# A two-layer hybrid decoder: x and mem handed over by channels, the first block's loads interleaved, and 512-wide token-major products

## The chip, the core and the metric

The kernel runs on one core of a Trainium2 chip. TensorE (PE) multiplies, VectorE (DVE), ScalarE (ACT) and GpSimd (POOL) work on tiles in SBUF and PSUM, and SyncE (SP) hands most loads and stores to the DMA queues. The metric is the device time of one execution in microseconds. The kernel before takes 1723.31 us, the median of three runs (1721.63 to 1724.03).

## The reference

The computation is a trunk of two layers over 512 tokens with 1024 channels. Each layer adds a mixer of the normalised h, and then a cross-attention to a memory of 256 tokens:

```
h = x
for l in range(DEPTH):
    un = _rmsnorm(h, mix_norm_g[l])
    h = h + _mixer_sublayer(un, ...)       # one projection w_in, four branches, gates, w_out
    xn = _rmsnorm(h, xa_norm_g[l])
    mn = _rmsnorm(mem, xa_mem_norm_g[l])
    h = h + _cross_attn(xn, mn, xa_wq[l], xa_wkv[l], xa_wo[l])
return _rmsnorm(h, final_norm_g)
```

The projection of a mixer is `z = un @ w_in`; its columns are cut into the inputs of RWKV-7 (r, k, v and low-rank codes), gated linear attention (GLA; q, k, v and a low-rank forget code of 16 columns behind v), retention (q, k, v) and a recurrent unit (LRU), and into the merge gates. `_rmsnorm` scales each token by `rsqrt(mean(x*x) + eps)` and each channel by a gain.

## The kernel before

**Layout.** h lives as eight tiles `hm` of 128 channels x 512 tokens. Every matrix and every activation that TensorE reads is split into two parts, a rounded one and the rest (`wh`, `wl` for weights; `uh`, `ul`, or `gh`, `gl`, for activations), and `mm3` (L309) issues three matmuls for one product: high x high (L313), and the two mixed ones (L314, L315). A weight is staged by an SP load into a tile `st`, ACT casts it into `wh` (L301), and DVE subtracts to make `wl` (L302). `wload` (L292) does that in two pieces per staged tile; three staged tiles fit at a time.

**Two ways of multiplying.** `proj` and `dense8` hold 128 weight columns in TensorE and stream 512 tokens. The token-major products hold 128 tokens and stream weight columns: `proj_tok` (L495) for the value inputs of GLA and retention (`gla_v`, `ret_v`), `v_proj` (L1321) for the values of the cross-attention, and `finish` (L1398) for the last `xa_wo` with the final norm. They stream 256 columns, in `gla_v` 264 (256 of v and 8 of the 16 code columns), so that a 512-column product is done in two halves, each with all eight channel blocks k.

**Start.** x arrives by tokens. SP loads ident (the unit matrix), the parameters, x's first 256 channels, the first staged weight, and on in turns. `first_rows` (L393) has TensorE transpose each channel block in four pieces (L414); ACT copies it with the gain into `uh` (L416), DVE makes the rest (L418) and the plain copy `hm` (L420), and ACT squares x and sums over channels for the token scale r. `bcast_cols` (L354) spreads r over the partitions: DVE multiplies it into ident (L359), TensorE multiplies that by `ones` (L361). In layer 0 that stands between the first and the second half of `gla_v`. The evacuations of `gla_v` (L520, L524 for the code columns) multiply by r as well. `flo_parts` (L528) transposes the code columns (L278, tile `m`). Then come `ret_v`, and the projections of the LRU in `mixers`.

**Layer 1.** h is there by channels; squares are summed on DVE, `rstd_finish` (L333) sums them over partitions on TensorE (L337) before `gla_v`.

**mem** is loaded by tokens in `load_mem` (L437), transposed by 16 matmuls on TensorE, scaled by its own r on DVE and written to a DRAM copy `mem_sc`, which the cross-attention of each layer reads back. h of each layer is written to DRAM (`h_sc`, eight stores) and read back for the residual after `w_out`.

**What sets the order.** A scheduler lays out the engines' queues from priorities: `tc.high_priority` pulls work ahead, `tc.issue_after(x)` holds an instruction's place behind x. In `rwkv_prep` (L940) long products of other branches are laid between the steps of a head pair j: `step(NST[i])` draws that many projections of 24 matmuls, and what follows is issued after the last of them. In a pair j the bonus (L1045, on `rkh` and `rkl` split by L322 and L323) comes first, then the transposes of v, then `step(NST[0])`.

## Time and profile before

| what | value |
|---|---|
| median of three runs | 1723.31 us |
| the profiled execution's own time | 1721.81 us |
| its span, first to last instruction | 1720.0 us |
| TensorE busy | 1692.2 us, 98% |
| DVE, ACT, POOL busy | 67%, 47%, 7% |
| data moved | 209 MB, 122 GB/s on average |

The profile's page gives each engine's busy time; its chain of work leads back from the last instruction to what released each step. The waits of an engine list its idle time by what ended it; windows give the busy time, the number of instructions (x) and the granted clock of stretches; a timeline lists single instructions with their start and length. Matmuls overlap, so the spacing from start to start, not the length of a row, is what one costs in a stream.

### The profile page before, as it was taken

Reading aid. Unit: us, or ns where it says so; the run is one execution under the profiler, and the core shown is the slowest. Engines: PE = TensorE matmul, PEld = TensorE weight load, DVE = VectorE, ACT = ScalarE, POOL = GpSimd, SP = SyncE. Lnnn points to the kernel's source line nnn. Section 1 sums busy time; section 2 is a strip of 40 time slices with the busy share of each in tenths; the row PEclk is TensorE's granted clock in tenths of the full one; section 3 lists DMA queues with packets and bytes.
Section 4 is the critical chain, followed back from the end, with each engine's and each line's share of the span. In section 5 each row is a group of like instructions: output and inputs, shape, how many; then the busy total and the mean of one; then the engine's idle time right before and its main releaser. Section 6 shows DMA issues by size and latency. Waiting matters only on the chain.

```text
span 1720.0 us, 27688 instructions
## 1 busy us (share of the span) xinstructions
PE 1692.2 (98%) x10570; PEld 1418.7 (82%) x10570; DVE 1147.7 (67%) x2369; ACT 810.0 (47%) x1539; POOL 114.2 (7%) x251
## 2 busy tenths in 40 slices
PE   7999999999999999999999999999999999999998
PEld 6987788877787788989898878887778878889898
DVE  7688577577775845756576737757878568557554
ACT  6494536454332334545446834545442234335354
POOL 1010000001003000000100100100110030000002
PEclk9999999999999999999999999999999999999999
DMA  6344325246562343424333424433547335334232
GB/s 218 98 134 124 99 81 165 88 114 173 159 174 88 118 155 99 135 87 130 108 102 87 128 73 137 123 93 104 152 131 210 99 96 186 92 97 134 86 104 81
DMA packets 320324, 209.17 MB, mean 122 GB/s; under 512 B 43616, under 2 KB 297792, under 8 KB 320192
## 3 DMA queue, kind: packets, MB, share of 16 engines
q1 hardware_dynamic: 310512, 189.71, 37.8%
q0 software_dynamic: 9680, 17.70, 3.6%
q8 instruction: 83, 1.36, 0.3%
q14 instruction: 49, 0.40, 0.1%
HBM read 176.97 MB, written 27.79 MB: 119 GB/s over the span
## 4 chain that ended last, share of the span: by engine, by line
PE 91%; DVE 6%; ACT 1%; DMA 1%; issue 1%; SPq 0%; POOL 0%; DVEq 0%; ACTq 0%; POOLq 0%
PE pb L313 25%; PE pb L315 25%; PE pb L314 25%; PE ps L278 2%; PE ps L313 2%; PE ps L315 2%; PE ps L314 2%; DVE wl L302 1%; PE ps L1069 1%; DVE sc L1037 1%; PE ps L1199 1%; PE ps L1205 1%; DVE sc L1036 1%; PE ps L784 1%; DVE R L1033 1%
## 5 line engine op out<-in xcount | busy, mean ns | idle before, releaser
L301 ACT CAST wh<-st 128x512 fp32r<-128x512 f32 (+1 forms) x548 | 339.6, 620 | 617.5 <-PE pb L314 502.8
L302 DVE TENSOR_TENSOR wl<-st,wh 128x512 fp32r<-128x512 f32 (+1 forms) x548 | 376.6, 689 | 339.3 <-ACT wh L301 300.1
L313 PE MATMUL pb<-uh,wh 128*128 128x512 f32 x1488 | 585.4, 394 | 0.0
L315 PE MATMUL pb<-uh,wl 128*128 128x512 f32 x1488 | 583.8, 392 | 0.0
L314 PE MATMUL pb<-ul,wh 128*128 128x512 f32 x1488 | 583.7, 392 | 0.0
L313 PEld LDWEIGHTS pb<-uh,wh 128*128 128x128 f32 x1488 | 280.1, 188 | 58.5 <-issue 1.6
L315 PEld LDWEIGHTS pb<-uh,wl 128*128 128x128 f32 x1488 | 279.6, 188 | 58.2 <-issue 0.3
L314 PEld LDWEIGHTS pb<-ul,wh 128*128 128x128 f32 x1488 | 279.7, 188 | 57.6 <-issue 0.8
L315 PE MATMUL pb<-yb,wl 128*128 128x512 f32 x256 | 101.3, 396 | 0.0
L313 PE MATMUL pb<-yb,wh 128*128 128x512 f32 x256 | 101.1, 395 | 0.0
L314 PE MATMUL pb<-yb,wh 128*128 128x512 f32 x256 | 100.1, 391 | 0.0
L315 PEld LDWEIGHTS pb<-yb,wl 128*128 128x128 f32 x256 | 48.0, 188 | 10.4
L313 PEld LDWEIGHTS pb<-yb,wh 128*128 128x128 f32 x256 | 48.1, 188 | 9.9
L314 PEld LDWEIGHTS pb<-yb,wh 128*128 128x128 f32 x256 | 48.1, 188 | 9.7
L914 DVE SCALAR_TENSOR_TENSOR bt<-bt,pb 128x512 f32<-128x512 f32 x48 | 32.9, 685 | 26.5 <-PE pb L315 26.2
L899 ACT ACTIVATE bt<-pb 128x512 f32<-128x512 f32 x64 | 38.0, 595 | 10.3 <-DVE hm L915 9.0
L313 PE MATMUL ps<-wh,R 128*128 128x256 f32 (+1 forms) x128 | 37.4, 292 | 0.2 <-DVE m L524 0.2
L314 PE MATMUL ps<-wl,R 128*128 128x256 f32 (+1 forms) x128 | 36.8, 288 | 0.0
L314 PE MATMUL pb<-wl,R 128*128 128x256 f32 (+1 forms) x128 | 36.7, 291 | 0.0
L314 PE MATMUL pb<-iv,wh 128*128 128x256 f32 x128 | 36.7, 286 | 0.0
L313 PE MATMUL pb<-wh,R 128*128 128x256 f32 (+1 forms) x128 | 36.5, 290 | 0.0
L313 PE MATMUL pb<-wh,uh 128*128 128x256 f32 x128 | 36.3, 284 | 0.0
(378 smaller groups left out, 2694.8 us busy)
## 6 DMA issues: line engine op xcount, KB each, us to landing
st<-in_w_in SPq DMA_DIRECT2D x154, 512.0 KB, 3.6
st<-in_w_branch SPq DMA_DIRECT2D x32, 512.0 KB, 3.5
st<-in_xa_wkv SPq DMA_DIRECT2D x32, 512.0 KB, 3.7
y_sc<-m POOLq DMA_DIRECT2D x32, 256.0 KB, 2.7
yb<-y_sc POOLq DMA_DIRECT2D x32, 256.0 KB, 4.9
st<-in_w_out SPq DMA_DIRECT2D x16, 512.0 KB, 3.5
st<-in_xa_wq SPq DMA_DIRECT2D x16, 512.0 KB, 3.4
st<-in_xa_wo SPq DMA_DIRECT2D x16, 512.0 KB, 4.0
```

Of the source, the lines that this page charges most:

```text
L278: PE.transpose(o, i, idn)
L301: S.copy(hi, st[:, i * n:(i + 1) * n])
L302: V.tensor_tensor(lo, st[:, i * n:(i + 1) * n], hi.bitcast(F32), op=ALU.subtract)
L313: PE.matmul(o, ah, bh, start=first and i == 0, stop=False)
L314: PE.matmul(o, ah, bl, start=False, stop=False)
L315: last_mm[0] = PE.matmul(o, al, bh, start=False, stop=last and i == n - 1)
L784: PE.matmul(ops[q][:, j], atts[q][:, j], v[:, b, h * P:(h + 1) * P], start=j == 0, stop=b == 0, skip_group_check=True)
L899: S.activation(t, o, AF.Tanh, scale=0.5)
L914: V.scalar_tensor_tensor(th[d], th[d], 1.0, o, op0=ALU.add, op1=ALU.mult)
L1033: V.scalar_tensor_tensor(dst[:, :, 1:], c8(kn[qs])[:, :, 1:], -1.0, c8(pp[qs])[:, :, :63], op0=ALU.mult, op1=ALU.mult)
L1036: V.scalar_tensor_tensor(b2[qs, :, q], c8(aa[qs]), 0.5, c8(cum[qs]), op0=ALU.mult, op1=ALU.mult)
L1037: V.tensor_tensor(b2[qs, :, 1 - q], c8(km[qs]), c8(cum[qs]), op=ALU.mult)
```

## The change

The host hands over x and mem transposed (`xt`, `memt`), so that the transposes of x (32) and of mem (16) and the copies out of PSUM fall away. At the start SP gives out the parameters, then in turns one channel block of x (256 KB, straight into its `hm` tile) and a piece of the first staged weights, cut by `FIRST_W`; ACT and DVE split them in the same order. ident and the constants come after these. While the data are on the way TensorE multiplies a tile of ones 11 times; its memset is POOL's first, ahead of the load of `heads`. The squares for r are taken after the splits, and r is made (`rstd_finish`) in the middle of the second half of `gla_v` in both layers; `proj_tok` evacuates both halves behind all its matmuls, and the spreading of r comes behind `proj_tok`. `tok_major` streams 512 columns for `ret_v`, `v_proj` and the first half of the last `xa_wo`. mem's scaling stands in `rwkv_prep`. h of layer 0 isn't written out: the residual is read from `xt`. `NST` has one projection of 24 matmuls ahead of the bonus, and four in place of five behind it. The tile `dec` is wider, which moves addresses only.

```diff
+FIRST_W = {0: 1, 1: 1, 2: 2, 4: 2, 6: 2}
-NST = (5, 1)
+NST = (1, 4, 1)
...
+        for k in range(KD):
+            n = FIRST_W.get(k)
+            if n:
+                nc.sync.dma_start(first_w[k // 4][:, k % 4:k % 4 + n], a["w_in"][0][k * P:(k + n) * P, ...
+            nc.sync.dma_start(xs[k], a["xt"][k * P:(k + 1) * P])
     cst = cp.tile([P, NCST], F32, name="cst")
+    nc.sync.dma_start(ident, a["ident"])
     nc.sync.dma_start(cst, a["consts"])
...
+    with tc.high_priority(offset=100000):
+        G.memset(ones, 1.0)
+        warm = pss((P, P))
+        for _ in range(11):
+            PE.matmul(warm, ones, ones, start=True, stop=True)
     heads = cp.tile([P, P + 134 + T], F32R, name="heads")
...
+    def tok_major(w, xh, xl, nb):
+        parts = [wload(w[q * 256:(q + 1) * 256], 2, T) for q in range(4)]
+        os_ = [pb() for _ in range(nb)]
+        for k in range(KD):
+            hi, lo = (x[k % 2] for x in parts[k // 2])
+            for b in range(nb):
+                bs = slice(b * P, (b + 1) * P)
+                mm3(os_[b], [(xh[k][:, bs], xl[k][:, bs], hi, lo)], first=k == 0, last=k == KD - 1)
+        return os_
...
+        with tc.high_priority(offset=100000):
+            for k in range(KD):
+                n = FIRST_W.get(k)
+                if n:
...
+                    chain("S", lambda: S.copy(wh[:, ws], st))
+                    chain("V", lambda: V.tensor_tensor(wl[:, ws], st, wh[:, ws].bitcast(F32), op=ALU.subtract))
+                chain("S", lambda: S.activation(hi[k], h[k], AF.Copy, scale=gcol[:, k:k + 1]))
+                chain("V", lambda: V.scalar_tensor_tensor(lo[k], h[k], gcol[:, k:k + 1], hi[k].bitcast(F32),
+                                                          op0=ALU.mult, op1=ALU.subtract))
+        acc = None
+        with tc.issue_after(last["S"].ins):
+            for k in range(KD):
+                acc = add_square(acc, h[k], T)
+        return hi, lo, lambda: rstd_finish(acc, T, D), parts
...
+            for bg in ((0, 1, 2), (3,)) if half else ((0, 1, 2, 3),):
+                os_ += [(pss if half else pb)((P, wd)) for _ in bg]
+                for k in range(KD):
+                    for b in bg:
+                        bs = slice(b * P, (b + 1) * P)
+                        mm3(os_[b], [(gh[k][:, bs], gl[k][:, bs], parts[k // 4][0][k % 4], parts[k // 4][1][k % 4])],
+                            first=k == 0, last=k == KD - 1)
+                    if half and k == 3 and callable(r):
+                        with tc.issue_after(last_mm[0].ins):
+                            r = r()
...
+                mm = step(NST[0])
                 bon = pss()
-                for x in (rkh, rkl):
-                    PE.matmul(bon, same, x, start=x is rkh, stop=x is rkl)
+                with tc.issue_after(mm):
+                    for x in (rkh, rkl):
+                        PE.matmul(bon, same, x, start=x is rkh, stop=x is rkl)
...
-        for k in range(KD):
-            nc.sync.dma_start(h_sc[l][:, k], h[k])
-        if l:
+        else:
+            for k in range(KD):
+                nc.sync.dma_start(h_sc[:, k], h[k])
             gh, gl, r = gain_split(h, g_)
-        rp = bcast_cols(r, T)
-        v_gla, ex = proj_tok(l, COL["gla_v"], gh, gl, r, extra=16, staged=(None, None) if l else first_w)
+            ready = None
+        v_gla, ex, r = proj_tok(l, COL["gla_v"], gh, gl, r, extra=16, ready=ready)
+        with tc.issue_after(last_mm[0].ins):
+            rp = bcast_cols(r, T)
         fl = flo_parts(ex)
         xh, xl = norm_split(h, g_, rp)
-        v_ret = proj_tok(l, COL["ret_v"], gh, gl, r)
+        for b, o in enumerate(tok_major(a["w_in"][l][:, COL["ret_v"]:COL["ret_v"] + T], gh, gl, 4)):
...
-            nc.sync.dma_start(old, h_sc[l][:, d])
+            nc.sync.dma_start(old, h_sc[:, d] if l else a["xt"][d * P:(d + 1) * P])
```

On TensorE the kernel before begins with the transposes of x (`R_73`, `R_74` are x's loaded tiles, `R_117` and `R_119` the two parts of x, `pb_259` and on the sums of the four token blocks):

```order
L1527 UNCONDITIONAL_BRANCH
L414 MATMUL ps_121<-ident,R_73 128x128 x4
L414 MATMUL ps_129<-ident,R_73 128x128 x4
L414 MATMUL ps_137<-ident,R_74 128x128 x4
L414 MATMUL ps_145<-ident,R_74 128x128 x4
L313 MATMUL pb_259<-wh_243,R_117 128x264
L314 MATMUL pb_259<-wl_244,R_117 128x264
```

In the changed kernel it begins with the multiplied ones (`R_131` and `R_133` are the two parts of x there, and L312 to L314 the three matmuls of `mm3`):

```order
L1552 UNCONDITIONAL_BRANCH
L222 MATMUL ps_105<-ones 128x128 x11
L312 MATMUL pb_195<-wh_135,R_131 128x264
L313 MATMUL pb_195<-wl_136,R_131 128x264
L312 MATMUL pb_196<-wh_135,R_131 128x264
L313 MATMUL pb_196<-wl_136,R_131 128x264
```

The products of ones stand where the transposes stood; nothing of x is needed for them.

At the end of `gla_v` and the start of `ret_v` the kernel before had 17 matmuls on TensorE between the first three transposes of the code columns (`m_241`, one per token block) and the fourth, of which these are the last:

```order
L315 MATMUL pb_568<-wh_550,R_119 128x256
L313 MATMUL pb_569<-wh_550,R_117 128x256
L314 MATMUL pb_569<-wl_551,R_117 128x256
L278 MATMUL ps_491<-ident,m_241 96x128
L315 MATMUL pb_569<-wh_550,R_119 128x256
```

In the changed kernel the spreading of r (L371) stands ahead of them, and the fourth transpose of the code columns (`m_193`) comes after four matmuls of `ret_v`:

```order
L371 MATMUL ps_440<-m_435,ones 128x512
L278 MATMUL ps_442<-ident,m_193 96x128 x3
L312 MATMUL pb_539<-wh_501,R_131 128x512
L313 MATMUL pb_539<-wl_502,R_131 128x512
L314 MATMUL pb_539<-wh_501,R_133 128x512
L312 MATMUL pb_540<-wh_501,R_131 128x512
L278 MATMUL ps_442<-ident,m_193 96x128
L313 MATMUL pb_540<-wl_502,R_131 128x512
```

DVE makes that fourth block of `m_193` in the last row of the following piece (L301 there makes `wl`, L536 and L540 are the evacuations of `gla_v`, the operations on `ti_657` small steps of `derive`, which makes constants from the parameters):

```order
L540 TENSOR_SCALAR m_193<-ps_317,ti_359 128x3x16
L268 TENSOR_SCALAR ti_657<-ti_657 128x4
L267 TENSOR_TENSOR ti_657<-ti_657,ti_656 128x4
L268 TENSOR_SCALAR ti_657<-ti_657 128x4
L267 TENSOR_TENSOR ti_657<-ti_657,ti_656 128x4
L301 TENSOR_TENSOR wl_502<-st_499,wh_501 128x512
L268 TENSOR_SCALAR ti_657<-ti_657 128x4
L301 TENSOR_TENSOR wl_506<-st_499,wh_505 128x512
L267 TENSOR_TENSOR ti_657<-ti_657,ti_656 128x4
L301 TENSOR_TENSOR wl_512<-st_509,wh_511 128x512
L536 TENSOR_SCALAR R_192<-ps_398,ti_359 128x248
L301 TENSOR_TENSOR wl_516<-st_509,wh_515 128x512
L540 TENSOR_SCALAR m_193<-ps_398,ti_359 128x3x16
```

In the kernel before the same place on DVE read:

```order
L524 TENSOR_SCALAR m_241<-ps_385,ti_221 128x3x16
L368 SCALAR_TENSOR_TENSOR m_541<-hm_116,par_78,ps_238 128x512
L302 TENSOR_TENSOR wl_551<-st_548,wh_550 128x512
L302 TENSOR_TENSOR wl_555<-st_548,wh_554 128x512
L520 TENSOR_SCALAR R_240<-ps_386,ti_221 128x248
L302 TENSOR_TENSOR wl_561<-st_558,wh_560 128x512
L302 TENSOR_TENSOR wl_565<-st_558,wh_564 128x512
L524 TENSOR_SCALAR m_241<-ps_386,ti_221 128x3x16
```

The four splits for `ret_v` stood there already, between the third and the fourth block of the code columns; the steps of `derive` stood behind these rows, and now stand ahead of and among them.

## Rows read from the trace of the kernel before

**Rows 1.** Page: busy by engine with share; the chain that ended last.

```profile
PE 1692.2 (98%) x10570; PEld 1418.7 (82%) x10570; DVE 1147.7 (67%) x2369; ACT 810.0 (47%) x1539; POOL 114.2 (7%) x251
PE 91%; DVE 6%; ACT 1%; DMA 1%; issue 1%; SPq 0%; POOL 0%; DVEq 0%; ACTq 0%; POOLq 0%
```

**Rows 2.** Waits of PE: line, what it waited for: us, times, longest.

```profile
PE ps L414 <- DMA R<-in_x: 8.0, 2, 7.0
PE ps L361 <- DVE m L359: 3.5, 1, 3.5
PE ps L1045 <- DVE m L323: 3.1, 7, 0.9
PE ps L1045 <- ACT m L322: 2.4, 4, 0.7
PE ps L337 <- POOL m L330: 0.9, 1, 0.9
```

**Rows 3.** Windows, start: PE, PEld, DVE, ACT, POOL busy (x); clock, DMA, GB/s.

```profile
7.00:11.50 4.50, 3.50 (x16) 3.12 (x17) 2.41 (x4) 2.73 (x5) 0.00 (x0) 1.00 1.10 353
...
13.50:25.90 12.40, 12.40 (x105) 12.30 (x103) 10.91 (x20) 11.21 (x42) 0.42 (x1) 1.00 0.96 306
25.90:29.60 3.70, 0.15 (x2) 0.07 (x1) 2.76 (x19) 3.50 (x4) 0.00 (x0) 1.00 0.85 269
29.60:33.80 4.20, 4.20 (x17) 3.63 (x18) 3.67 (x8) 2.81 (x6) 0.00 (x0) 0.59 0.70 198
...
44.30:55.90 11.60, 11.60 (x100) 11.60 (x99) 8.80 (x34) 3.92 (x8) 0.00 (x0) 1.00 0.49 136
55.90:67.50 11.60, 11.60 (x99) 11.60 (x98) 5.27 (x9) 4.41 (x9) 0.00 (x0) 1.00 0.33 92
```

**Rows 4.** Windows of later stretches, columns as in Rows 3.

```profile
72.00:152.00 80.00, 80.00 (x358) 65.88 (x357) 68.61 (x112) 64.81 (x95) 5.29 (x10) 1.00 0.40 112
590.00:690.00 100.00, 100.00 (x443) 82.80 (x442) 57.70 (x94) 38.88 (x67) 0.00 (x0) 1.00 0.42 129
1672.50:1710.50 38.00, 38.00 (x319) 38.00 (x319) 16.64 (x40) 16.84 (x45) 9.87 (x12) 1.00 0.16 52
```

**Rows 5.** Timeline of SP's issues at the start: start, length.

```profile
1.67 0.43 SPq L198 DMA_DIRECT2D R<-in_x  x1
```

**Rows 6.** Timeline of ACT, start; in brackets the idle time before.

```profile
8.42 1.16 ACT L301 CAST wh<-st 128x528 fp32r<-128x528 f32 x2 [6.39 <-DMA st<-in_w_in]
...
11.10 0.69 ACT L416 ACTIVATE R<-ps,par 128x512 fp32r<-128x512 f32 x1 [0.34 <-PE ps L414]
```

**Rows 7.** Timeline of DVE beside `ret_v`, layer 0.

```profile
48.34 0.69 DVE L302 TENSOR_TENSOR wl<-st,wh 128x512 fp32r<-128x512 f32 x1
...
49.34 0.16 DVE L267 TENSOR_TENSOR ti<-ti,ti 128x4 f32<-128x4 f32 x1
49.54 0.17 DVE L268 TENSOR_SCALAR ti<-ti 128x4 f32<-128x4 f32 x1
```

**Rows 8.** Timeline of PE in retention, layer 0: four f32 matmuls, two records each.

```profile
237.69 1.16 PE L784 MATMUL ps<-R,m 128*128 128x128 f32 x8
```

**Rows 9.** Timeline of PE: the sum for r in layer 1 (four f32 matmuls).

```profile
869.24 1.05 PE L337 MATMUL ps<-ones,m 128*128 128x1 f32 x8 [0.89 <-POOL m L330]
```

**Rows 10.** Timeline of PE: the bonus of j = 0, layer 0.

```profile
328.05 0.50 PE L1045 MATMUL ps<-m,heads 128*128 128x512 f32 x1 [0.52 <-ACT m L322]
```

**Rows 11.** Timeline of PE: transposes of mem between matmuls, two of eight pairs.

```profile
251.58 0.38 PE L278 MATMUL ps<-ident,hm 128*128 128x128 f32 x2
251.72 0.48 PE L313 MATMUL pb<-uh,wh 128*128 128x512 f32 x1
...
252.50 0.42 PE L278 MATMUL ps<-ident,hm 128*128 128x128 f32 x2
```

**Rows 12.** Window in GLA, layer 0, columns as in Rows 3.

```profile
166.90:170.30 3.40, 3.40 (x15) 2.30 (x14) 1.45 (x5) 0.00 (x0) 0.00 (x0) 0.50 0.00 0
```

More of the change, by code (lines that the diff above doesn't have):

```diff
@@ L192, in trunk_kernel @@
     ident = cp.tile([P, P], F32, name="ident")
-    with tc.high_priority(offset=100000):
-        nc.sync.dma_start(ident, a["ident"])
-    xs = [Rt((P, 4, 256)) for _ in range(4)]
-    def load_x(i):
-        nc.sync.dma_start(xs[i], a["x"][:, i * 256:(i + 1) * 256].rearrange("(b p) d -> p b d", p=P))
-    with tc.high_priority(offset=100000):
-        load_x(0)
+    xs = [ht() for _ in range(KD)]
     par = [cp.tile([P, NPAR], F32, name=f"par{l}") for l in range(depth)]
@@ L229, in spread @@
         return heads[:, (j + 1) * P + 134:(j + 2) * P + 134]
-    ones = cp.tile([P, P], F32, name="ones")
-    G.memset(ones, 1.0)
     reset = cp.tile([P, T], F32, name="reset")
@@ L406, in chain @@
                 last[eng] = f()
-            return last[eng]
-        for k in range(KD):
-            uh, ul = gh[k // 4][:, k % 4], gl[:, k] if k < 4 else yb()
-            with tc.high_priority(offset=100000):
-                tp = pss()
-                for b in range(4):
-                    chain("PE", lambda: PE.transpose(
-                        tp[:, b * P:(b + 1) * P], xs[k // 2][:, b, (k % 2) * P:(k % 2 + 1) * P], ident))
-                acts.append(chain("S", lambda: S.activation(uh, tp, AF.Copy, scale=gcol[:, k:k + 1])))
-            with tc.high_priority(offset=WPRI - 500):
-                chain("V", lambda: V.scalar_tensor_tensor(ul, tp, gcol[:, k:k + 1], uh.bitcast(F32), op0=ALU.mult,
-                                                          op1=ALU.subtract))
-                chain("V", lambda: V.tensor_copy(hT[k], tp))
-            hi.append(uh)
-            lo.append(ul)
@@ L504, in proj_tok @@
             G.memset(ex, 0.0)
+        halves = []
         for half in range(2):
             c0 = half * wd
-            n = min(wd, T - c0)
-            parts = [wload(w_in[q * 512:(q + 1) * 512, col + c0:col + c0 + wd], 4, wd, None if half else staged[q])
-                     for q in range(2)]
-            os_ = [(pss if half else pb)((P, wd)) for _ in range(4)]
-            for k in range(KD):
-                for b in range(4):
-                    bs = slice(b * P, (b + 1) * P)
-                    mm3(os_[b], [(gh[k][:, bs], gl[k][:, bs], parts[k // 4][0][k % 4], parts[k // 4][1][k % 4])],
-                        first=k == 0, last=k == KD - 1)
+            parts = ready if ready and not half else \
+                [wload(w_in[q * 512:(q + 1) * 512, col + c0:col + c0 + wd], 4, wd) for q in range(2)]
+            os_ = []
+            for bg in ((0, 1, 2), (3,)) if half else ((0, 1, 2, 3),):
[8 more added lines that the diff above has]
+                            r = r()
+            halves.append(os_)
+        for half, os_ in enumerate(halves):
+            c0 = half * wd
+            n = min(wd, T - c0)
             for b in range(4):
@@ L1050, in rwkv_prep @@
                 for w in range(4):
-                    transpose(ta[:, w], vt[:, w * P:(w + 1) * P], ident)
+                    with tc.issue_after(mm):
+                        transpose(ta[:, w], vt[:, w * P:(w + 1) * P], ident)
                 s0, s1 = c8(sv[:, j % 2, 0]), c8(sv[:, j % 2, 1])
@@ L1273, in step @@
             return last_mm[0].ins
-        rwkv_prep()
+        rwkv_prep(mem_scale)
         rwkv_invert()
```

145 lines of the change are left out of this document (70 added, 75 removed).

## The prediction

> **What bounds the kernel now.** I read the page first, then TensorE's waits, then windows of the stretches that the change touches, and single instructions in a timeline where a size was missing. TensorE is busy for 1692.2 us of a span of 1720.0, and the chain that ended last lies on it for 91% [rows 1]. All its recorded waits of some size are few: 8.0 us for x at the start, 3.5 for the spreading of r between the halves of `gla_v`, 5.5 in eleven waits for the bonus, 0.9 for the sum for r in layer 1 [rows 2]. So a change gains what it takes off TensorE's queue, in matmul time or in these waits, and nothing elsewhere, unless it brings a new wait. Busy time hides one more loss, half speed: the 16 transposes of x took 3.50 us, 0.22 each, while a pair of such transposes amid mem's projections adds about 0.24 (below); and behind the wait of 3.55 us the granted clock is 0.59 over 4.2 us, in which 17 matmuls ran where 36 would at the 105 in 12.4 us of the stretch before [rows 3]. The profiled execution took 1721.81 us, 1.5 below the median of the runs; I make the sum against 1721.8.
>
> **A. The start, up to the LRU's projection at 67.5 us.** Before: transposes from 7.03, the first matmul of `gla_v` at about 11.5, its first half to 26, the wait, r's spreading, the second half to 44.3, `ret_v` to 67.5 [rows 2, 3]. After, step by step.
>
> *First data.* SP gave out the first block of x at 1.67 and PE had it at 7.03 [rows 2, 5], behind ident, parameters and 512 KB. The new first block, parameters, 132 KB of weights and 256 KB of x, is 190 KB less, which at 353 GB/s [rows 3] is 0.5 us: 6.5 at the latest. If the time from issue to landing halves with the block, it is 4.4. I take 5.3. ACT's copy with gain costs 0.69 [rows 6], so data are ready at 6.0.
>
> *Multiplied ones.* 11 f32 matmuls need no data. Four such in full speed take 1.16 us [rows 8], 0.29 each, and twice that at half speed: 3.2 or 6.4 us in all. From about 1.5 us (an estimate: POOL's memset comes just before) they end at 4.7 to 7.9. Since PE came from idling here as it did at 7.03 and at 29.6, I take mostly half speed, 7.2. That is later than the data, and costs about 1 us; in turn the matmuls behind start near full speed.
>
> *First half.* 96 matmuls of 264 columns, at 12.4/105 = 0.118 [rows 3]: 11.3 us, to 18.5 (17.3 to 19.6). Per channel block that is 1.42 us of TensorE against 388 KB, 1.10 us at 353 GB/s, and ACT's 0.69 for x and, per block, half to all of a cast of 0.58 [rows 6]: TensorE is the slowest of the three, though not by much.
>
> *Sum for r in the second half.* 1.05 us [rows 9] of TensorE, new in layer 0; its squares, eight on ACT behind the last split, should end some 3 us before it is wanted. Second half: 11.3 more, to 30.8. The wait of 3.5 us and the half speed behind it are gone, because the spreading of r comes behind `proj_tok`: 0.85 us (an estimate from two 512-wide matmuls at 0.226 [rows 4] and transposes of code columns), to 31.7 with the code columns at 32.0.
>
> *A new wait.* The fourth transpose of the code columns now has four matmuls of `ret_v` ahead of it, not 17. DVE makes its data behind four splits of 0.69, an evacuation and the steps of `derive` at 0.2 each [rows 7]. If DVE starts these steps when r is known and the constants have been looked up on ACT, at about 26, its queue stands at 32.8 for the first split and at 36 for the fourth block. PE waits 0.5 to 4 us; I take 2.5. Behind PE's wait stands all of `ret_v`.
>
> *`ret_v`.* 96 matmuls of 512 columns at 100.0/443 = 0.226 [rows 4]: 21.7 us where 192 of 256 took 23.2 [rows 3]. So the LRU starts at 32.0 + 2.5 + 21.7 = 56.2: **11.3 us gained.** With the best of each piece it is 15; with the worst, and the half speed of rows 3 once more behind the new wait (2.1 us), 6.4.
>
> **B. 512 columns in the four other places** (`ret_v` of layer 1, `v_proj` of both layers, half of the last `xa_wo`). Each is 96 matmuls of 512 in place of 192 of 256. The stretch of 256-wide ones ran at 38.0/319 = 0.119, the 512-wide at 0.226 [rows 4]: two narrow ones cost 0.0125 more than a wide one, 1.2 us a place, 4.8. In `v_proj` both sums now end together, so the evacuations of the last one bunch; I take off 0.5: **4.3** (1 to 5). The weights' bytes and casts are the same. ACT and DVE have slack there (57.7 and 38.9 of 100 us busy [rows 4]).
>
> A rule speaks against this. The Trainium skill, page "TensorE: Matmul & The Clock Gate", section "Back-to-back issue gap", gives 262 cycles for 256 columns and 518 for 512; two narrow ones would then lose 6 cycles, 2.5 ns, and a place 0.24 us. The trace doesn't agree for the narrow ones (119 ns, not 109). If only the stretch at 1672 us were slow for a reason of its own, the sum would come out by the page's rule; that is a rival below.
>
> **C. The bonus of j = 0.** By the order, 48 long matmuls stand ahead of it in place of 37 and 13 behind it in place of 24; for j = 1 to 3 nothing moves. One wait there was 0.52 [rows 10], the second product adds its own, and a quarter of 5.5 us [rows 2] is 1.4 for both layers: **1.4** (0 to 2). The 11 matmuls moved ahead take 2.5 us, more than any one wait of 0.9.
>
> **D. mem's transposes.** From one pair to the next it is 0.92 us with three long matmuls between, 0.68 at 0.226: 0.12 a transpose [rows 4, 11]. Sixteen: **1.9**.
>
> **E. r in layer 1.** The wait of 0.9 [rows 2] goes, since the sum stands some 130 matmuls later: **1.0** (0.5 to 1.3); the sum's own 1.05 stays.
>
> **At nothing:** the eight stores of h in layer 0 and the residual from `xt` (DMA share 0.4 [rows 4], and both ends of them far from any wait); ident and the constants behind x (wanted at some 23 us); mem's scaling in `rwkv_prep` (eight DVE steps of 0.3 to 0.7 us; the copy is read hundreds of us later; without cover they would cost 3); `heads` 0.2 us later; `dec`.
>
> **Sum:** 11.3 + 4.3 + 1.4 + 1.9 + 1.0 = 19.9, so 1721.8 - 19.9 = **1701.9** (1703.4 if counted from the median of the runs). With the ends of the ranges: 1697 to 1711.
>
> **Rivals.** *The new wait at its worst, with half speed behind it:* A is 6.4, 1706.8. For it: the order on DVE; against: one may find `derive`'s steps long done. *The loads come no earlier* (smaller blocks in turns need as long as one large one, since all queues share 353 GB/s already [rows 3]), so the change doesn't do what it says at the start: the first block at 7.0 as before and blocks in the pace of loads of 1.10 to 1.5 us; A is about 9, 1704.2. *Narrow ones cost no more than half of wide ones* (the gap of 0.0125 us isn't the width's): B is 1.0 and A 1.0 less, 1706.2; that is the page's rule above. *The gain is given back behind:* between 72 and 152 us DVE is busy for 68.6 of 80 us and ACT for 64.8 [rows 4], PE never waits, but all of the squares, splits and loads come 11 us closer together; if DVE was only just ahead there, PE waits for weights, and A comes to nothing: 1713, and worse if the stretch costs 5 more. *Better than I think:* 15 for A, no wait in C, and the half speed in GLA at 167 us (clock 0.50 over 3.4 us [rows 12]) not met again, 1.7: 1721.8 - 15 - 4.3 - 2 - 1.9 - 1.0 - 1.7 = 1696. *Slower:* TensorE stays at half speed through the start, because waits for blocks recur. Each us of half speed costs 0.5. `gla_v`'s 192 matmuls would take 0.22 in place of 0.118, 19.6 more, and `ret_v` 21.7 more: 1743. It turns the sign from some 40 us of half speed, of the 50 there are. Against it: in the trace full speed came back within 4.2 us of steady matmuls after the wait of 3.5 [rows 3].
>
> **How the numbers follow.** Forecast 1701.9 (own range 1697 to 1706): 0.60. New wait at its worst, 1707: 0.14. Loads no earlier, 1704: 0.08. Width without gain, 1706: 0.05. Given back, 1713: 0.05, of it 0.02 within 0.2%. Better, 1696: 0.05. Half speed, 1743: 0.03. A difference of 0.2%, 3.4 us, is about what a measurement of this kernel can tell from no change. Faster by more than that: 0.95; within: 0.02; slower: 0.03. The range 1695 to 1710 leaves out the half speed, most of the given back and the tails.
>
> **What would show it.** A: the first `mm3` on PE at 6 to 8 us, 96 matmuls in about 11.4 us behind it, no gap between the halves, a wait of PE at the fourth transpose of code columns (for DVE, 0.5 to 4 us), the first LRU matmul at 56 us. A first matmul after 8.5, or gaps of PE for x or weights between blocks, would show the loads as the bound. B: 96 wide matmuls in 21.7 us each time. C: no wait at the bonus of j = 0, the others as before. D: no transposes of `hm` near 250 us. E: no wait at the sum in layer 1. It would be wrong if the granted clock fell in the start, if waits for `wl` showed up from 60 to 150 us, or if POOL, DVE or ACT were found ahead of PE in places where the trace of before has none.

## The result

The changed kernel takes **1702.79 us**, the median of four runs (1701.36 to 1705.67), beside 1723.67 us of the kernel before on the same chip (1721.63 to 1725.10). The ratio is 0.9882, 95% interval 0.9864 to 0.9900: faster by 1.2%, inside the range of 1695 to 1710 and within 1 us of the forecast 1701.9. The profiled execution took 1701.36 us, with a span of 1699.6 us against 1720.0.

The page's first line and its chain, which answer to [rows 1]: TensorE works 13 us less and is busy for 99% of the shorter span; of the chain that ended last it has 88%, DVE 7%.

```profile
PE 1679.0 (99%) x10072; PEld 1388.9 (82%) x10072; DVE 1142.6 (67%) x2344; ACT 805.3 (47%) x1496; POOL 113.5 (7%) x251
...
PE 88%; DVE 7%; ACT 2%; DMA 1%; issue 1%; SPq 0%; DVEq 0%; ACTq 0%
```

TensorE's waits in the changed kernel (line, what it waited for: us, times, longest), which answer to [rows 2]:

```profile
PE ps L1065 <- DVE m L333: 4.8, 8, 0.9
PE pb L312 <- ACT R L423: 1.6, 1, 1.6
PE ps L1065 <- ACT m L332: 1.3, 2, 0.7
PE ps L986 <- ACT m L332: 1.3, 2, 0.7
PE ps L278 <- DVE m L540: 1.1, 1, 1.1
PE ps L222 <- POOL ones L218: 1.0, 1, 1.0
```

The wait for x (8.0 us) has shrunk to 1.0 + 1.6; those for the spreading of r and for the sum for r in layer 1 are gone. The waits for the bonus (now L1065) are as large as before, 6.1 against 5.5. Two are new: 1.1 for the code columns (L278), which the prediction had, and 1.3 at L986, which it had not. L986 is the sum of squares of RWKV's keys in `rwkv_prep`, and it waits for ACT's part of a split, a rounded copy from which DVE then makes the rest.

To see where time went, I read the start of a few matmuls that both kernels have from each profile's timeline, and take the distances. The marks are, in each layer, the first matmul of GLA's gate (L612 in the changed kernel), the last of retention (L806), the first that spreads the norms of the keys in `rwkv_prep` (L1039) and the first of `rwkv_invert` (L1162); "RWKV's pairs" lies between the last two. The rows below the second are runs of the next section. Lengths in us; the last column is the span:

| kernel | start to GLA's gate | GLA, retention | to spreading in RWKV | RWKV's pairs | to GLA's gate, layer 1 | GLA, retention | to spreading | RWKV's pairs | to the end | span |
|---|---|---|---|---|---|---|---|---|---|---|
| before | 116.8 | 124.2 | 77.8 | 192.9 | 453.5 | 120.8 | 74.3 | 192.9 | 366.8 | 1720.0 |
| changed | 105.3 | 121.2 | 76.1 | 192.9 | 450.4 | 120.9 | 75.0 | 192.9 | 364.9 | 1699.6 |
| changed, again | 105.1 | 124.3 | 76.9 | 193.0 | 450.4 | 120.9 | 75.1 | 193.0 | 364.9 | 1703.4 |
| narrow | 107.7 | 124.5 | 76.0 | 193.0 | 452.7 | 120.8 | 74.3 | 193.0 | 367.0 | 1708.9 |
| bonus as before | 105.2 | 124.1 | 76.5 | 192.9 | 450.4 | 120.9 | 74.7 | 193.0 | 365.0 | 1702.8 |
| mem by tokens | 106.4 | 124.1 | 78.7 | 192.9 | 450.3 | 120.9 | 76.2 | 192.9 | 365.1 | 1707.6 |

So the gain of 20.4 us of span is 11.5 in the start, 3.0 in layer 0's GLA, 1.7 up to RWKV, 3.1 between the layers, 1.9 at the end, and minus 0.7 ahead of RWKV in layer 1. RWKV's pairs, in which the bonus lies, gave nothing. The 3.0 in GLA was not in the sum, only in the rival "better than I think"; the first experiment is about it.

TensorE's timeline at the start of the changed kernel (start, length, in brackets the idle time before):

```profile
1.00 4.12 PE L222 MATMUL ps<-ones 128*128 128x128 f32 x22 [1.00 <-POOL ones L218]
6.76 0.39 PE L312 MATMUL pb<-wh,R 128*128 128x264 f32 x1 [1.64 <-ACT R L423]
...
10.46 0.39 PE L314 MATMUL pb<-wh,R 128*128 128x264 f32 x1 [0.28 <-DVE R L424]
...
23.42 0.95 PE L347 MATMUL ps<-ones,m 128*128 128x1 f32 x8
...
31.60 1.03 PE L371 MATMUL ps<-m,ones 128*128 128x512 f32 x2
32.47 0.49 PE L278 MATMUL ps<-ident,m 128*96 128x128 f32 x3
...
34.99 0.31 PE L278 MATMUL ps<-ident,m 128*96 128x128 f32 x1 [1.11 <-DVE m L540]
...
56.01 0.39 PE L312 MATMUL pb<-uh,wh 128*128 128x512 f32 x1
```

The ones end at 5.1, the first product of `gla_v` starts at 6.76 behind ACT, r's sum (23.42) and its spreading (31.60) stand amid matmuls without a wait, and the LRU starts at 56.01, where it started at 67.5. In windows (busy time and instructions of PE, PEld, which is TensorE's loading of the stationary tile, DVE, ACT, POOL; clock, DMA share, GB/s), to set beside [rows 3]:

```profile
6.76:19.06 12.30, 12.02 (x97) 11.81 (x98) 11.41 (x18) 11.56 (x20) 0.42 (x1) 1.00 1.00 345
19.06:31.60 12.54, 12.54 (x106) 12.54 (x105) 9.60 (x45) 8.27 (x16) 0.00 (x0) 1.00 0.38 108
32.70:56.00 23.30, 22.19 (x100) 18.09 (x99) 19.20 (x38) 11.03 (x19) 0.00 (x0) 1.00 0.43 124
```

In the first window all three engines and the loads are all but full (ACT 11.56, DVE 11.41 of 12.30, 345 GB/s): the first half of `gla_v` lies near three bounds at once.

### The profile page after: what moved, and what is told of

Its sections match the earlier page's. It is cut to its first block, busy times and chain, and to the rows that moved or that the text cites. A ratio compares the mean times of both kernels' runs of the same rounds, so it can differ in the third digit from the quotient of the medians.

```text
span 1699.6 us, 26626 instructions
## 1 busy us (share of the span) xinstructions
PE 1679.0 (99%) x10072; PEld 1388.9 (82%) x10072; DVE 1142.6 (67%) x2344; ACT 805.3 (47%) x1496; POOL 113.5 (7%) x251
## 4 chain that ended last, share of the span: by engine, by line
PE 88%; DVE 7%; ACT 2%; DMA 1%; issue 1%; SPq 0%; DVEq 0%; ACTq 0%
PE pb L312 25%; PE pb L314 25%; PE pb L313 25%; DVE wl L301 2%; PE ps L278 2%; PE ps L312 1%; PE ps L314 1%; PE ps L313 1%; ACT wh L300 1%; PE ps L1090 1%; DVE sc L1055 1%; PE ps L1220 1%; PE ps L1226 1%; DVE R L1051 1%; PE ps L800 1%
## 5 line engine op out<-in xcount | busy, mean ns | idle before, releaser
L301 DVE TENSOR_TENSOR wl<-st,wh 128x512 fp32r<-128x512 f32 (+1 forms) x544 | 374.6, 689 | 332.9 <-ACT wh L300 294.2
L312 PE MATMUL pb<-uh,wh 128*128 128x512 f32 x1488 | 585.2, 393 | 0.0
L314 PE MATMUL pb<-uh,wl 128*128 128x512 f32 x1488 | 583.0, 392 | 0.0
L312 PEld LDWEIGHTS pb<-uh,wh 128*128 128x128 f32 x1488 | 280.1, 188 | 58.6 <-issue 1.4
L314 PEld LDWEIGHTS pb<-uh,wl 128*128 128x128 f32 x1488 | 279.5, 188 | 58.7 <-issue 0.3
L314 PE MATMUL pb<-yb,wl 128*128 128x512 f32 x256 | 101.3, 396 | 0.0
L312 PE MATMUL pb<-yb,wh 128*128 128x512 f32 x256 | 101.2, 395 | 0.0
L314 PEld LDWEIGHTS pb<-yb,wl 128*128 128x128 f32 x256 | 48.1, 188 | 10.4
L312 PEld LDWEIGHTS pb<-yb,wh 128*128 128x128 f32 x256 | 48.1, 188 | 9.9
L312 PE MATMUL pb<-wh,R 128*128 128x512 f32 (+1 forms) x128 | 43.2, 338 | 1.6 <-ACT R L423 1.6
L313 PE MATMUL pb<-wl,R 128*128 128x512 f32 (+1 forms) x128 | 43.1, 337 | 0.0
L314 PE MATMUL pb<-wh,R 128*128 128x512 f32 (+1 forms) x128 | 42.7, 337 | 0.3 <-DVE R L424 0.3
L314 PE MATMUL pb<-sc,wl 128*128 128x256 f32 x128 | 36.2, 283 | 0.0
L312 PE MATMUL pb<-sc,wh 128*128 128x256 f32 x128 | 36.2, 283 | 0.0
```

The lines of the kernel that those rows point to most:

```text
L301: V.tensor_tensor(lo, st[:, i * n:(i + 1) * n], hi.bitcast(F32), op=ALU.subtract)
L312: PE.matmul(o, ah, bh, start=first and i == 0, stop=False)
L313: PE.matmul(o, ah, bl, start=False, stop=False)
L314: last_mm[0] = PE.matmul(o, al, bh, start=False, stop=last and i == n - 1)
```

## The experiments

Each kernel is the changed one with the edit shown, and was run beside the kernel before.

**The changed kernel again.** No edit.

> The changed kernel once more, beside the others of this call. In its first profile the granted clock did not fall in layer 0's GLA, while it did in the kernel before and in four variants of the changed one that share every instruction there, at a cost of 2.9 us. Theory: that fall comes and goes between executions of one kernel and is no effect of the change; here the span is either near 1699.7 or near 1702.5, and the profiled execution shows which goes with it. Rival: the change removed it, and the four variants brought it back by their different start; then this run shows full clock there again, as the first.

1705.35 us, ratio 0.9896 (0.9873 to 0.9920). The windows of layer 0's GLA, first in the changed kernel's first profile, with the clock behind POOL's column:

```profile
150.00:156.00 6.00, 5.39 (x67) 3.52 (x66) 5.95 (x18) 3.72 (x5) 1.10 (x2) 1.00 0.63 176
156.00:160.00 4.00, 4.00 (x33) 2.85 (x33) 1.60 (x4) 0.75 (x4) 0.00 (x0) 1.00 0.33 131
160.00:164.00 4.00, 4.00 (x39) 3.10 (x38) 0.00 (x0) 2.13 (x11) 0.60 (x2) 1.00 0.02 4
```

and in this run of the same program:

```profile
150.00:156.00 6.00, 5.18 (x66) 3.53 (x66) 5.93 (x18) 3.72 (x5) 1.11 (x2) 1.00 0.65 176
156.00:160.00 4.00, 4.00 (x20) 3.11 (x20) 1.59 (x4) 0.00 (x0) 0.00 (x0) 0.52 0.32 131
160.00:164.00 4.00, 4.00 (x23) 2.60 (x22) 0.00 (x0) 1.81 (x10) 0.60 (x2) 0.62 0.02 4
```

The same instructions, once at full clock (2.4 GHz) and once at 0.52, that is at half of it (1.2 GHz) for nearly all of the window, behind a stretch in which PE is idle for 0.6 and 0.8 of 6 us. The rival (the change removed the fall) is out: the fall comes and goes between executions of one program. It costs 3.1 us here (124.3 against 121.2). The kernel before had it in its profile [rows 12]. With the fall in both, the change gains 1720.0 - 1703.4 = 16.6 us. Of the 3.8 us by which the first comparison shows more, 3.1 are the clock and 0.8 a shorter wait at the keys' sum of squares in layer 0 (0.7 us there, 1.5 in this run); both differ between executions of one program, so they are luck. The fastest execution of the kernel before that was measured beside any of these kernels took 1717.81 us, 16.5 more than the changed kernel's fastest, 1701.36.

**Without the multiplied ones.**

```diff
-        warm = pss((P, P))
-        for _ in range(11):
-            PE.matmul(warm, ones, ones, start=True, stop=True)
```

> The changed kernel without its 11 multiplied ones at the start; nothing else differs. Theory: in the profile of the changed kernel the first product of gla_v began at 6.76 us, after a wait of 1.6 us for ACT's first part of x, so the products of ones delay nothing; what they give is the clock. Without them the first matmuls of gla_v run at half speed (0.22 in place of 0.12 us each) for some 5 us, so the LRU's projection starts 2 to 3.5 us later than at 56.0, and the time is 2 to 3.5 us longer. Rival: the ones give nothing (matmuls of gla_v come up to speed by themselves, or the loads are the bound of the first half): within 0.7 us of the changed kernel.

1703.52 us, ratio 0.9890 (0.9874 to 0.9907); GLA's gate at 106.1, 0.8 to 1.0 behind the changed kernel's two. The theory's 2 to 3.5 is out; the rival's 0.7 holds nearly. The timeline of its first matmuls:

```profile
6.75 0.59 PE L309 MATMUL pb<-wh,R 128*128 128x264 f32 x1 [6.75 <-ACT R L420]
7.13 0.42 PE L310 MATMUL pb<-wl,R 128*128 128x264 f32 x1
```

They begin at the same 6.75 and run at half speed (0.22 from start to start further on) until 9.9, which costs some 1.4 us (an estimate: 14 matmuls at 0.10 more each); the changed kernel runs at full speed there, but in its first profile loses part of that in a wait (10.46 above). And the ones do not bring full speed each time. Of twelve profiles of kernels that have them, seven run the first block at full speed and five at half speed up to 10.2 to 10.8, the kernel "narrow" for one:

```profile
1.01 5.06 PE L222 MATMUL ps<-ones 128*128 128x128 f32 x22 [1.01 <-POOL ones L218]
7.00 0.59 PE L312 MATMUL pb<-wh,R 128*128 128x264 f32 x1 [0.92 <-ACT R L423]
7.38 0.42 PE L313 MATMUL pb<-wl,R 128*128 128x264 f32 x1
```

Those five reach GLA's gate about 1.2 us later than the seven where nothing else differs (106.4 against 105.0 to 105.3). Beside 106.1 without the ones, they gain 0.8 to 1.1 us where they bring full speed and lose 0.3 where they don't, with one profile of the kernel without them.

**256 columns in place of 512.**

```diff
-    def tok_major(w, xh, xl, nb):
-        parts = [wload(w[q * 256:(q + 1) * 256], 2, T) for q in range(4)]
-        os_ = [pb() for _ in range(nb)]
+    def tok_major(w, xh, xl, nb, c):
+        parts = [wload(w[q * 512:(q + 1) * 512, c * 256:(c + 1) * 256], 4, 256) for q in range(2)]
+        os_ = [(pss if c else pb)((P, 256)) for _ in range(nb)]
...
```

> The changed kernel with 256 streamed columns in the five places that stream 512 (ret_v twice, v_proj twice, half of the last xa_wo): twice as many matmuls, weights loaded in the shapes of the kernel before. Theory: two narrow matmuls cost 0.0125 us more than a wide one, 1.2 us for 96 pairs, so 5 to 6 us longer in all, 1.2 of it in ret_v of each layer. Rival: a narrow matmul costs about half a wide one (the page's cycles: 0.24 us a place), 1 to 2 us longer. A third: the wider shape changed how early weights come, and the difference is not in the spacing of matmuls but in waits.

1710.43 us, ratio 0.9931 (0.9916 to 0.9946), 5.4 to 6.9 above the three other kernels that ran beside it. By stage: the start is 1.2 longer than in "mem by tokens", which shares its half speed there; between the layers 2.3 more (`v_proj` and `ret_v`), at the end 2.1 more (`v_proj` and `xa_wo`): 5.6 in five places, 1.1 each. The windows amid `ret_v`, of "narrow" and then of the changed kernel:

```profile
37.50:55.00 17.50, 17.50 (x148) 17.50 (x147) 16.19 (x31) 9.54 (x18) 0.00 (x0) 1.00 0.40 105
```

```profile
36.00:55.00 19.00, 19.00 (x85) 15.73 (x85) 15.13 (x30) 9.37 (x17) 0.00 (x0) 1.00 0.43 125
```

17.5/148 = 0.118 and 19.0/85 = 0.224: two narrow ones cost 0.013 us more than a wide one. PEld is full in the narrow stretch (17.50 of 17.50) and not in the wide one (15.73 of 19.00), so the loads of the stationary tile are the likely bound of the narrow form; that is read, not tried.

The Trainium skill, page "TensorE: Matmul & The Clock Gate", section "Back-to-back issue gap", gives 262 and 518 cycles for the two widths, by which the five places would cost 1.2 us (an estimate: 6 cycles a pair at 2.4 GHz). The runs don't agree with the Trainium skill's cycles: 0.118 us for 256 columns where these make 0.109, and 0.224 for 512 where they make 0.216.

**The bonus as before, and one projection later.**

```diff
-                mm = step(NST[0])
                 bon = pss()
-                with tc.issue_after(mm):
-                    for x in (rkh, rkl):
-                        PE.matmul(bon, same, x, start=x is rkh, stop=x is rkl)
+                for x in (rkh, rkl):
+                    PE.matmul(bon, same, x, start=x is rkh, stop=x is rkl)
...
-                mm = step(NST[1])
+                mm = step(5)
```

> The changed kernel with the bonus as in the kernel before: no projection ahead of it, five behind. Theory: the wait at the bonus of j = 0 (1.1 us in both kernels) is for DVE's rest of the split, which the scheduler sets behind that pair's whole preparation; moving the bonus by 11 matmuls of TensorE's queue moved only what stands between its first and its second product, so going back changes nothing: within 0.5 us, the wait again in two parts of about 0.6 and 0.3 at j = 0 of both layers. Rival, my forecast: the move takes 0.7 us off each layer, so going back costs 1.4 us.

The second kernel has `NST = (2, 3, 1)`.

> The changed kernel with two projections (48 matmuls) ahead of the bonus and three behind. Theory: the second product of the bonus keeps its place on TensorE, where the scheduler thinks DVE's split done, and DVE's split stands no earlier; the wait of some 1.1 us at j = 0 stays in each layer: within 0.5 us of the changed kernel. Rival: one more projection of 5.4 us covers what was short: about 2 us less.

1704.76 us (ratio 0.9904, 0.9889 to 0.9918) and 1705.06 us (0.9901, 0.9886 to 0.9915). RWKV's pairs take 192.9 to 193.0 us in both layers of both kernels, as in the kernel before and in the changed one. The theory holds. The waits of TensorE for the bonus, of "bonus as before":

```profile
PE ps L1063 <- DVE m L333: 3.0, 6, 0.9
PE ps L1063 <- ACT m L332: 2.4, 4, 0.7
```

and of the one with two projections ahead:

```profile
PE ps L1065 <- DVE m L333: 5.3, 8, 1.1
PE ps L1065 <- ACT m L332: 1.3, 2, 0.7
```

As more work goes ahead, the wait changes its name from ACT to DVE and keeps its size or grows a little: 5.4, 6.1 in the changed kernel, 6.6. The changed kernel's timeline at j = 0 of layer 0, PE and then DVE:

```profile
317.19 0.39 PE L312 MATMUL pb<-uh,wh 128*128 128x512 f32 x1
318.50 0.50 PE L1065 MATMUL ps<-m,heads 128*128 128x512 f32 x1 [0.93 <-DVE m L333]
```

```profile
317.04 0.69 DVE L1055 TENSOR_TENSOR sc<-m,m 64x512 f32<-64x512 f32 x1
317.76 0.69 DVE L333 TENSOR_TENSOR m<-m,m 128x512 fp32r<-128x512 f32 x1
```

The bonus needs two products. The first, on ACT's part, was moved; the second waits for DVE's rest (L333), which stands last in the pair's preparation (it starts 0.03 us after L1055 ends). In the kernel before it stood there too, and so did the second product: 28 matmuls of TensorE lay between first and second, 17 in the changed kernel, 5 in the one with two projections ahead.

**Mem by tokens.**

```diff
-            nc.sync.dma_start(mT[i], a["memt"][2 * i * P:(2 * i + 2) * P].rearrange("(k p) m -> p k m", p=P))
+            nc.sync.dma_start(ms[i], a["mem"][(i // 2) * P:(i // 2 + 1) * P, (i % 2) * T:(i % 2 + 1) * T])
...
+                transpose(tp[:, b * P:(b + 1) * P], ms[2 * b + k // 4][:, (k % 4) * P:(k % 4 + 1) * P], ident)
+            V.tensor_copy(mT[k // 2][:, k % 2], tp)
```

> The changed kernel with mem handed over by tokens as in the kernel before: 16 transposes on TensorE and eight copies on DVE again, the scaling left in its new place. Theory: 16 x 0.12 = 1.9 us more between retention's end and the first bonus in layer 0; elsewhere nothing. Rival: part of it is hidden, because a wait near it (at the sum of squares of the keys, 0.7 us) shrinks by as much: 1.2 us.

One run of 1709.44 us. The stage from retention to RWKV's spreading is 78.7 us, against 76.9 in the changed kernel's second profile, 1.8 more, and 76.1 in its first, 2.6 more; without the waits of TensorE in that stage (1.1, 1.5 and 0.7) it is 2.1 to 2.2 more than either. In layer 0 the theory holds and the rival doesn't. The theory's "elsewhere nothing" is not what came: in layer 1, where no transpose of mem stands, the stage is 1.2 longer (76.2 against 75.0 and 75.1), because TensorE waits 1.8 us at the keys' sum of squares in place of 0.6 and 0.7; that wait is taken up below.

**The weights whole.**

```diff
-FIRST_W = {0: 1, 1: 1, 2: 2, 4: 2, 6: 2}
+FIRST_W = {0: 4, 4: 4}
...
```

> The changed kernel with the first weights loaded whole (528 KB ahead of x's first block, 528 KB ahead of its fifth), not in turns with x. Theory: 396 KB more stand ahead of the first block of x, 1.1 us at 353 GB/s, and another 132 KB's worth of splits on ACT and DVE ahead of its part; the first matmul of gla_v comes 1.1 to 2 us later than at 6.7, and since all bytes are the same and the loads are nearly the bound, part of it is made up by the end of the first half (19.1 us): the LRU starts 0.5 to 2 us later. Rival: the order of loads within a full queue changes nothing, within 0.3.

One run of 1709.68 us. The first product, from its timeline:

```profile
7.55 0.59 PE L312 MATMUL pb<-wh,R 128*128 128x264 f32 x1 [2.37 <-ACT R L423]
```

The first is at 7.55, where the other eleven with the ones have it from 6.76 to 7.21. The block runs at half speed, so it is compared with the others that do: GLA's gate is at 106.86 against 106.42 and 106.45 in two of them. That is 0.4 us, between the theory's 0.5 to 2 and the rival's 0.3, while profiles of one program lie 0.2 apart there: the interleaving counts for less than half a microsecond, and one profile shows no more. Of the rest of its time 3 us are luck: the clock fell in layer 1's GLA too (124.2 and 123.9 in the two layers).

**r between the halves.**

```diff
-                    if half and k == 3 and callable(r):
+                    if not half and k == KD - 1 and callable(r):
```

> The changed kernel with r made between the two halves of gla_v (in both layers), not in the middle of the second. Theory: the first half ends at 19.1 us and the squares' sum is done at about 22.8, so PE waits 3.7 to 4 us in layer 0, and behind that wait runs at half speed for some 4 us, which costs 2 more; in layer 1 nothing. LRU's projection 5.5 to 6.5 us later than in the changed kernel, the time as much longer. Rival: without half speed 3.7 to 4.

1710.87 us, ratio 0.9928 (0.9906 to 0.9949); GLA's gate at 111.0, 5.7 behind. The theory holds. PE's timeline, then the windows behind the wait, with the clock (0.50 and 0.73):

```profile
23.23 1.86 PE L347 MATMUL ps<-ones,m 128*128 128x1 f32 x8 [3.85 <-DVE m L340]
```

```profile
23.00:27.00 4.00, 3.77 (x17) 3.77 (x18) 1.06 (x14) 1.79 (x4) 0.00 (x0) 0.50 0.56 165
27.00:31.00 4.00, 4.00 (x27) 4.00 (x26) 3.66 (x23) 2.08 (x4) 0.00 (x0) 0.73 0.00 0
```

The wait is 3.85 us; behind it the engine is given half speed, which by the clock costs 3.1 more (0.50 and 0.27 of 4 us each); and the wait for the code columns, 1.1 in the changed kernel, isn't among this one's waits. That makes 5.8, where 5.7 was measured. Moving one step by 36 matmuls saved that: it is half of what the start gained, and the edit doesn't touch the layout of x.

**The code columns late.**

```diff
-        fl = flo_parts(ex)
         xh, xl = norm_split(h, g_, rp)
...
+        with tc.issue_after(last_mm[0].ins):
+            fl = flo_parts(ex)
         derive(l)
```

> The changed kernel with the transposes of the code columns behind all of ret_v in place of ahead of and among it. Theory: the wait of 1.1 us at the fourth transpose, and some 0.2 us of cold restart, go, and nothing waits for the codes before GLA; the LRU's projection starts 1.1 to 1.4 us earlier than in the changed kernel. Rival: DVE's queue is what is short there, and PE waits for the weights' splits in ret_v instead; within 0.4 us.

1704.26 us, ratio 0.9893 (0.9866 to 0.9920). GLA's gate is at 103.9, 1.1 to 1.4 earlier: the theory holds. At the gate nothing is late; but in GLA it has the fall of the clock (125.6), so the time shows none of it.

**The splits first.**

```diff
+                with tc.high_priority(offset=HOFF):
+                    V.scalar_tensor_tensor(rk, rt, dc("h_rk", j), km, op0=ALU.mult, op1=ALU.mult)
...
+                with tc.high_priority(offset=HOFF):
+                    split(rkh, rkl, rk)
```

(the same around the split of the keys' squares; HOFF is 1500)

> The changed kernel with a higher priority for the splits that feed the bonus and the sum of squares of the keys (and for the step ahead of the bonus's split). By the order DVE then makes the bonus's rest 3 places earlier at j = 0, 1 to 8 at the others, and ACT's part of the keys' split stands ahead of the small casts; but the scheduler also draws TensorE's products forward with them, by 6 to 22 matmuls. Theory: since the product follows the place where the scheduler thinks the split done, the waits at the bonus (6.1 us in the profile of the changed kernel) fall by less than 1 us, and the time is within 1.5 us of the changed kernel's. Rival: the waits are DVE's order alone; they go by half, 3 us less.

1700.42 us, ratio 0.9878 (0.9854 to 0.9901) where the late code columns and the changed kernel again, which ran beside it, have 1704.26 and 1705.35, with intervals that overlap. RWKV's pairs take 191.6 in place of 192.9 in each layer; the stage ahead of them is 76.7 in layer 0, between the changed kernel's two profiles (76.1 and 76.9), and 76.0 in layer 1, 0.9 to 1.0 longer. Its waits:

```profile
PE ps L1069 <- DVE m L334: 2.6, 4, 0.8
PE ps L987 <- ACT m L333: 2.3, 2, 1.4
PE ps L1069 <- ACT m L333: 1.4, 2, 0.7
```

The bonus waits 4.0 in place of 6.1, so the theory's "less than 1 us" was wrong there; the sum of squares (L987) did not gain by its own splits' priority, with 2.3 against 1.3 and 2.2 in the changed kernel's two profiles. In layer 1 the split that it waits for (1.4 us) stands on ACT behind a wait of 1.56 us for a load of the low-rank codes. The time is within 1.5 us of the changed kernel's undisturbed one, but by a loss that I had not placed.

**Two versions that gather this.** The first has the late code columns, the priority for the bonus's split alone, and RWKV's low-rank codes behind the products of keys and r:

```diff
-            for i, n in enumerate(("rw_w2", "rw_a2")):
-                raw = mt()
...
             if mem_scale is not None:
                 mem_scale()
+            for i, n in enumerate(("rw_w2", "rw_a2")):
+                raw = mt()
...
```

> A version made from what the runs showed: the changed kernel with the code columns' transposes behind ret_v, a higher priority for the step and the split ahead of the bonus, and the low-rank codes of RWKV (two small loads, a table load of ACT and five of its casts) behind the keys' and r's products, so that they no longer stand ahead of ACT's split for the keys' sum of squares. Theory: 1.3 us at the start, 0.8 to 1.3 in each layer at the bonus, 0.6 to 1.5 in each layer at the sum of squares; some 4 to 6 us less than the changed kernel in undisturbed stretches, 1696 to 1699 us. Rival: the work that is moved back makes a wait where the decay is prepared, before the bonus of j = 0, and gives back the 1 to 3 us there.

1701.84 us, ratio 0.9885 (0.9857 to 0.9912), above the 1696 to 1699 of the theory. The rival came true in part, at another place: in layer 0 the sum of squares now waits for DVE. DVE itself was idle for 1.56 us there until ACT's part of the split came, which started at 253.23, where ACT had worked without a pause since 245.81.

```profile
PE ps L968 <- DVE m L334: 2.0, 1, 2.0
```

That stage takes 78.9 us, 2.0 more than in the changed kernel's second profile. The wait is only 0.5 longer than the 1.5 there; behind it the clock is 0.50 from 254.87 to 258.28, in which 9 matmuls ran where 17 ran in the 3.72 us behind, and that is most of the 2.0. In layer 1 the stage takes 74.3, 0.8 less, without a wait at the sum of squares. So the second version moves the codes in layer 1 alone:

> The version before it, but with the low-rank codes moved back in layer 1 alone; in layer 0 they stand where the changed kernel has them, since the move made a wait of 2.0 us for DVE there. Theory: of the changed kernel's waits 1.3 us go at the start, about 0.9 in each layer at the bonus, and 1 to 2 at the sum of squares in layer 1: some 4 us less than the changed kernel in stretches at full clock, the fastest execution at a span of 1695.5 to 1697.5, its median around 1700 because of the clock in GLA. Rival: the gains at single waits are taken back by others as in the version before it; within 2 us of the changed kernel.

1700.16 us (1697.17 to 1702.35), ratio 0.9862 (0.9844 to 0.9881). Its span of 1697.2 is 2.4 below the changed kernel's, both with full clock in GLA, and its fastest is 1695.4. The forecast had 1695.5 to 1697.5 for the fastest span and around 1700 for the median. It is faster than the kernel before; against the changed kernel the intervals overlap, so that the gain is shown by the stages (191.6 and 191.7 us for RWKV's pairs, 74.5 ahead of them in layer 1, but 76.7 ahead of them in layer 0) and not by the times.

## Why the prediction was right, step by step

**A, the start: right in sum (11.5 of 11.3), wrong in pieces that cancel.** The ones ended at 5.1, not 7.2, and the data were later than thought, 6.76 and not 6.0; the first half ended at 19.06, not 18.5, because 97 instructions took 12.3 us and TensorE waited 0.28 for DVE. r's sum cost 0.8 from start to start (1.05 forecast) and its spreading with the first code columns 1.1 (0.85 and 0.3 forecast). The new wait was there, at the place named and for DVE, but 1.1 and not 2.5: DVE came to the fourth block at 34.67, where the estimate had 36. The wait between the halves and the half speed behind it is the largest piece, 5.7 by the experiment that put r back; `ret_v`'s width gave 1.2. The remaining 4.6 or so belong to the layout of x, its loads and the ones together, by subtraction: the start with x by tokens and nothing else changed was not run.

**B, 512 columns: right.** 5.6 us in five places, 4.4 in four (4.3 forecast); the rule by the Trainium skill's cycles, 1.2 in five, is out.

**C, the bonus: wrong.** The step "48 long matmuls stand ahead of it in place of 37" looked at the first of two products. The second kept its place behind DVE's last step, and the wait went there. It measured 0.0 in place of 1.4: the two waits at j = 0 of layer 0 were 0.52 and 0.14 before, and are 0 and 0.93 now. The order had shown it: the distance between the two products shrank by the 11 matmuls by which the first moved.

**D, mem's transposes: right as a term** (1.8 to 2.6 for 1.9, 2.1 to 2.2 without the waits), but the stage gained 1.7 in one profile and 0.9 in the other, because of a wait that the prediction hadn't. It names, as what would make it wrong, "if POOL, DVE or ACT were found ahead of PE in places where the trace of before has none", and one such place came: the keys' sum of squares. PE's wait in layer 0, and ACT's queue ahead of it, both in the changed kernel:

```profile
257.49 0.50 PE L986 MATMUL ps<-m,heads 128*128 128x512 f32 x1 [0.69 <-ACT m L332]
```

```profile
252.68 1.28 ACT L969 ACT_TABLE_LOAD   x1
...
254.51 0.60 ACT L964 CAST iv<-m 128x512 fp32r<-128x512 f32 x1
...
255.54 1.26 ACT L976 CAST iv<-m 64x512 fp32r<-64x512 f32 x2
256.82 0.62 ACT L332 CAST m<-m 128x512 fp32r<-128x512 f32 x1
```

A table load and the casts of the low-rank codes stand ahead of the split for which PE waits. In the kernel before the first such split (L322 there) stood ahead of all of these casts (L948 and on) and of the table load, which came at 275.29, and PE hardly waited (0.17 in all):

```profile
272.06 0.62 ACT L322 CAST m<-m 128x512 fp32r<-128x512 f32 x1
272.58 0.62 ACT L948 CAST iv<-m 128x512 fp32r<-128x512 f32 x1
```

The prediction went by TensorE's order and not by ACT's. What turned the two around is shown by the run with mem by tokens: with the transposes back, and the scaling left in its new place, ACT's split again starts ahead (256.59) of the first cast of the codes (257.30) and the table load (257.94). That the order alone makes layer 0's wait is not shown: that run still waits 1.1 us at the sums of squares, and the first of the two versions above, with the codes moved away, 2.0. In layer 1 the order is that of the kernel before, and the wait (0.6) comes from two small loads ahead of those casts:

```profile
1091.79 0.62 ACT L964 CAST iv<-m 128x512 fp32r<-128x512 f32 x1 [0.19 <-DMA m<-in_rw_w]
...
1093.25 0.62 ACT L964 CAST iv<-m 128x512 fp32r<-128x512 f32 x1 [0.32 <-DMA m<-in_rw_a]
```

That this is the cause in layer 1 is supported by the versions that move the codes (there the stage falls from 75.0 to 74.3 and 74.5; the kernel before has 74.3), and by the other profiles: PE doesn't wait in "narrow" (74.3), where ACT doesn't wait for the loads; it waits 0.4 to 0.9 us where ACT waits 0.3 to 0.8 for them, and 1.4 to 1.8 in the three kernels where ACT waits 1.4 to 1.8 (without the ones, mem by tokens, the splits first). Why the loads land later there I did not find out.

**E: right** (between the layers 3.1 us came of the 3.2 that B and E put there).

**The sum:** without the clock in GLA the changed kernel gains 20.4 - 3.0 = 17.4 in the first profile and 16.6 in the second, where 19.9 was forecast. Missing are C's 1.4 and 1 to 2 us of waits at the sums of squares. That the profile's gain of 20.4 came out within 0.5 of the forecast is luck: the fall of the clock, in the profile of before and not in that of after, filled the gap; the prediction had it as a part of "better", at 1.7. The lower ends of the terms add up to 9.8, which makes 1712 for the end of the ranges and not 1711.

The rivals: the wait at its worst did not come; the loads did come earlier, though 0.7 us less so than thought; nothing was given back behind the start (in GLA, at an equal clock, 124.2 and 124.3); half speed through the whole start did not come, though five profiles had it up to 10.2 to 10.8.

## What to carry to other kernels

A step that an engine must wait for is cheapest where work of that engine surrounds it: moving r's sum into the second half of a product saved 5.7 us, more than is left for the whole new layout of x. When a consumer is moved away from a wait, look at each of its operands and at the place of the last one's producer: here, moving the product of the first operand by 11 or by 23 matmuls gained nothing. And before a profile is set against another, compare the granted clock by stage, since one execution's luck (3 us here) is larger than three of the five terms of this sum.

## What was not expected of the hardware

The same program had full clock in layer 0's GLA in one profile and 0.52 to 0.62 over 8 us in another. Of the fourteen profiles ten have that fall and four don't, and TensorE's idle time about there (44.5 to 50.5 us behind GLA's gate) doesn't tell them apart: 0.58 to 0.84 us in the ten, 0.57 to 0.93 in the four. In layer 1 the like happened in two of fourteen (123.9 in place of 120.9). After 11 products of ones, which ended 0.7 to 2.4 us ahead of the first data, the first block ran at full speed in seven profiles and at half speed in five. Two 256-column matmuls cost 0.013 us more than one of 512, at 0.118 and 0.224 each.
